# Stick-breaking heads with queries on the partitions: a backward scan on VectorE in place of triangular matmuls on TensorE

## The chip, the cores and the metric

The kernel runs on one core of one Trainium2 chip. The metric is device time in microseconds of one execution; three runs of the kernel before gave 1107.64, 1107.03 and 1107.19 us, and the median, 1107.19 us, stands for it.

## The reference, cut to what matters

One layer of a hybrid encoder, for 256 tokens of width 2048, all in float32. Eight forgetting-attention heads and eight stick-breaking heads (128 wide each) share one input projection; their outputs are normed per group and projected back; then a convolutional FFN follows (up-projection to 2 x 5632, causal depthwise convolution, SiLU gate, down-projection). The change touches the stick-breaking heads alone:

```python
def stick_breaking_attention(q, k, v):
    # beta[t,s] = sigmoid(q_t.k_s/sqrt(d)); A[t,s] = beta[t,s] * prod_{s<j<t}(1-beta[t,j]), s < t
    z = jnp.einsum('bhqd,bhkd->bhqk', q, k) * HEAD_DIM ** -0.5
    mask = k_pos[None, :] < q_pos[:, None]
    log_beta = jax.nn.log_sigmoid(z)
    log_one_minus = jnp.where(mask, log_beta - z, 0.0)
    suffix = lax.cumsum(log_one_minus, axis=key_axis, reverse=True) - log_one_minus
    weights = jnp.where(mask, jnp.exp(log_beta + suffix), 0.0)
    return jnp.einsum('bhqk,bhkd->bhqd', weights, v)
```

Each query needs, for every key, the sum of softplus(z) over all later keys up to the query. Which axis lies on the partitions decides how that sum can be taken.

## The kernel before, in words

**Arithmetic.** Every large product is made of three matmuls: a float32 matrix is split into a rounded high part and a low remainder, and high x high, high x low and low x high are summed. So each 1 MB tile of weights (128 x 2048 per tile) is loaded by a DMA into `w_raw`, its high part is written by ScalarE (`w_hi`, line 201), and its low part by VectorE (`w_lo`, line 202), before TensorE multiplies with both. `w_hi` and `w_lo` have two buffers each in the first half of the kernel, so ScalarE can write a new `w_hi` only when TensorE has read the one two tiles back.

**Order.** A projection is a run of such blocks: 24 matmuls for `token_major` (lines 231 to 241), 32 for `from_features`. After each block the host-side `step()` (line 181) advances the first two generators in the queue `waiting`; each generator is one head, cut into pieces by its `yield`s. So the small work of the heads is recorded between the blocks of whichever projection runs then. A scheduler places the recorded instructions on the engines in the section up to line 790, and each engine then works through its own queue in order.

**The forgetting heads** (`fox_head`, line 591) have queries on the partitions: scores in `ps_s`, softmax, and in a later piece three transposes by TensorE into `ps_p` (line 624), which are evacuated by ScalarE twice (lines 627 and 628) and by VectorE once (629) to make the weights `pT`; then `weighted` (line 575) multiplies with the values into `ps_o`, and `attended` (line 336) scales and splits `ps_o` into `oT` and adds its squares to `ssq`.

**The stick-breaking heads** (`sb_head`, line 701; heads 0 to 7 in this text) have keys on the partitions. The scores `ps_z` take three matmuls of 256 columns for the first 128 keys and one of 128 for the last 128 keys (lines 707 and 708). ScalarE makes log(1+exp(-|z|)) in three steps (712 to 714), VectorE makes softplus `sp` (718, 719), both split it (721, 722). After a `yield`, four matmuls with a constant triangle and a constant of -1 (lines 727 and 728) add minus the sum over later keys to the scores in place; ScalarE takes the exponential (730), and the result is already transposed the way `weighted` wants it; it is masked and split (732 to 736). After a second `yield` comes `weighted`. Two `yield`s, three pieces.

**Banks and buffers that tie the pieces together.** `ps_s`, `ps_z` and `ps_p` share one pool of two buffers (`pss`). `ps_o` shares a pool of two (`psb`, tag `t`) with `pg` (line 775, the sum of squares for a group's norm). The accumulators of all projections share a pool of two (`psa`, tag `acc`). The values of the second half of the stick-breaking heads, heads 4 to 7, are projected into one of these accumulators and then evacuated by `values` (line 522): ScalarE writes `vB` and `vBt` (line 292), VectorE writes `vBlo` (line 526). `vB`, `vBlo` and `vBt` have one buffer each, so they cannot be written before `weighted` of head 3 has read the values of heads 0 to 3.

**What runs beside the heads.** Heads 0 to 3 run under the value projection of the second half and the first blocks of the output projection; heads 4 to 7 under the output projection of the first group (`w_out`, lines 762 to 789, four column groups c = 0 to 3 of two blocks each). `finish()` (line 765) drains the heads before the second group. The output projection's c = 1 takes the accumulator that held the values of heads 4 to 7. The last `w_out` blocks are followed by the FFN, whose order is written out by hand.

Of the kernel before, what the change touches and what calls it, by code (L numbers as in the profile page):

```python
# [8 lines left out]
F32 = mybir.dt.float32  # L9
# [5 lines left out]
P = 128  # L15
D = 2048
S = 256
# [12 lines left out]

C_ID, C_TRI, C_ONE = (P * i for i in range(3))
C_MF = 3 * P
C_MS, C_NTRI, C_NONE = (C_MF + P * i for i in range(1, 4))
C_COLS = C_MF + 4 * P

AHEAD = 200
WINDOW = 2
# [8 lines left out]
def hybrid_layer(  # L46
# [31 lines left out]
    def f32(t):  # L78
        return t.bitcast(F32)
# [198 lines left out]
    with ExitStack() as actx:  # L278
# [200 lines left out]
        mask2, limit2 = (  # L479
            f32(masksR[:, i * P : (i + 1) * P]).unsqueeze(1).to_broadcast([P, 2, P]) for i in range(2)  # L480
        )
        limit = f32(masksR[:, P : 2 * P])
        gq = const.tile([P, 1], F32, name="gq")
        dve.tensor_scalar(gq, g_q, QSCALE, None, op0=ALU.mult)

# [99 lines left out]
        def weights_tiles(name):  # L585
# [2 lines left out]
                tmp.tile([P, P], F32, name=f"{name}1", tag="pT1"),  # L588
            )

        def fox_head(h, qT, kT, first):
            while any(g in waiting for g in first):
                yield
            yield
            ps = pss.tile([P, 3, P], F32, name="ps_s", tag="s")
            s0, s1 = ps[:, 0, :], ps[:, 1:3, :].rearrange("p a b -> p (a b)")
            j = h % 4
            nc.tensor.matmul(s0, qT[0][0][:, j, :], kT[0][0][:, j, :], start=True, stop=False)
# [23 lines left out]
            pt = pss.tile([P, 3, P], F32, name="ps_p", tag="s")  # L622
            for i in range(3):
                nc.tensor.transpose(pt[:, i, :], pr[:, i, :], ident)
            pT, pT1 = weights_tiles("pT")
            pt0 = pt[:, 0:2, :].rearrange("p a b -> p (a b)")
            act.copy(pT[:, 0], pt0)
            act.copy(pT1, pt[:, 2, :])
            dve.tensor_tensor(pT[:, 1], pt0, f32(pT[:, 0]), op=ALU.subtract)
            yield  # L630
            attended(weighted(vA, slice(h * HD, (h + 1) * HD), (pT, pT1)), h, g_fox, 0)

        for half in range(2):
            if half:
# [20 lines left out]
        def sb_heads(c0, scale, parts):  # L655


            heads = []
            for i in range(0, 4, 2):
                acc = feature_major(wi, c0 + i * P, psa, "acc")  # L660
                t2 = summed(tmp, acc, "t2", bufs=1)
                dve.scalar_tensor_tensor(
                    t2, t2, scale, R1.unsqueeze(1).to_broadcast([P, 2, S]), op0=ALU.mult, op1=ALU.mult
                )
                full, hi, lo = parts(i)
                some = t2[:, :, : hi.shape[2]]
                act.copy(hi, some)
                act.copy(full, t2[:, :, P:])
# [7 lines left out]
        def sb_queries(half):  # L676
            places = []

            def parts(i):
                if not places:  # L680

                    assert scored[:4] == [0, 1, 2, 3]
                    lows = last_rows("q1_low", 2) if half else [low[:, 0, 4 * P * j : 4 * P * (j + 1)] for j in range(2)]
                    places.extend((full_tile(f"qB{half}_1"), high_tile(f"qB{half}"), lows))
                full, hi, lows = places
                return full[:, i : i + 2, :], hi[:, i : i + 2, :], lows[i // 2].rearrange("p (h s) -> p h s", h=2)

            return sb_heads(B0 + 512 * half, QSCALE, parts)

        def sb_keys(half):  # L690
            places = []

            def parts(i):
                if not places:
                    two = last_rows("k1_parts", 2) if half else [low[:, 0, 4 * P * j : 4 * P * (j + 1)] for j in (2, 3)]
                    places.extend((full_tile(f"kB{half}_1"), *(of_four(t) for t in two)))
                return tuple(o[:, i : i + 2, :] for o in places)

            return sb_heads(B0 + WF + 512 * half, 1.0, parts)

        def sb_head(h, qT, kT, v):
            (q1, *q), (k1, *k) = qT[h % 4], kT[h % 4]
            ps = pss.tile([P, 3, P], F32, name="ps_z", tag="s")
            z0, z1 = ps[:, 0:2, :].rearrange("p a b -> p (a b)"), ps[:, 2, :]
            zz = ps.rearrange("p a b -> p (a b)")
            mm = nc.tensor.matmul
# [4 lines left out]
            e = tmp.tile([P, 3 * P], F32, name="e", tag="pr")  # L711
            act.activation(e, zz, AF.Abs)
            act.activation(e, e, AF.Exp, scale=-1.0)
            act.activation(e, e, AF.Ln, bias=1.0)
            sp = tmp.tile([P, 3, P], F32, name="sp", tag="sp", bufs=1)
            diagonal = sp[:, 0::2, :]
            sp = sp.rearrange("p a b -> p (a b)")
            dve.scalar_tensor_tensor(sp, zz, 0.0, e, op0=ALU.max, op1=ALU.add)
            dve.tensor_tensor(diagonal, diagonal, limit2, op=ALU.min)
            sps = tmp.tile([P, 2, 3 * P], F32R, name="sps", tag="sps")  # L720
            act.copy(sps[:, 0, :], sp)
            dve.tensor_tensor(sps[:, 1, :], sp, f32(sps[:, 0, :]), op=ALU.subtract)
            yield

            for i in range(2):
                s = sps[:, i, :]
                mm(zz, ntri[:, :P], s, start=False, stop=False, skip_group_check=True)
# [381 lines left out]
def _constants():  # L1109
# [4 lines left out]
    c[:, C_ID : C_ID + P] = i == j  # L1114
    c[:, C_TRI : C_TRI + P] = i <= j
    c[:, C_ONE : C_ONE + P] = 1.0
    c[:, C_NTRI : C_NTRI + P] = np.where(i >= j, -1.0, 0.0)
    c[:, C_NONE : C_NONE + P] = -1.0
    c[:, C_MF : C_MF + P] = np.where(j > i, BIG, 0.0)
    c[:, C_MS : C_MS + P] = np.where(i >= j, 0.0, -BIG)  # L1120
    return c


# [30 lines left out]
```

## Time and profile before

| what | value |
|---|---|
| median of three runs | 1107.19 us (1107.03 to 1107.64) |
| span of the profiled execution | 1104.9 us |
| TensorE (PE) busy | 1099.6 us, 100% |
| VectorE (DVE) busy | 870.4 us, 79% |
| ScalarE (ACT) busy | 706.3 us, 64% |
| GpSimd (POOL) busy | 44.0 us, 4% |
| DMA moved | 246.09 MB, mean 223 GB/s |
| stick-breaking heads | from about 264 to 346 us of the span |

The span is that of one execution taken by the hardware profiler, from its first instruction to its last; the run's own time is 2.3 us longer than the span at the median. Busy shares are averages over all stages. TensorE matmuls are pipelined, so their records overlap; the time a group takes on TensorE is read from the start of its first record to the start of what follows.

### The profile page before, as it was taken

The numbers are of one execution on the slowest core, as the hardware profiler recorded it, in microseconds if no ns is written. First come the engines' busy times: TensorE is split into PE (matmuls) and PEld (weight loads), VectorE is DVE, ScalarE is ACT, GpSimd is POOL, SyncE is SP. The second block draws the span as 40 slices with busy tenths as digits, with TensorE's granted clock in tenths as the row PEclk, the third lists the DMA queues.
The fourth block names the chain that finished last, engine by engine and source line by source line (L and its number), as shares of the span: only waits on it lengthen the run. The fifth ranks groups of instructions, "written<-read, shape, count | busy, mean of one in ns | idle before, by whom it ended". The sixth has DMA issues, their size and how long they took to land. (4 is left out here: it accounts for less than half of the span.)

```text
span 1104.9 us, 14836 instructions
## 1 busy us (share of the span) xinstructions
PE 1099.6 (100%) x5880; PEld 953.9 (86%) x5880; DVE 870.4 (79%) x941; ACT 706.3 (64%) x879; POOL 44.0 (4%) x44
## 2 busy tenths in 40 slices
PE   9999999999999999999999999999999999999998
PEld 7998888888888888888888888888888888888887
DVE  6755767667676677679889888889798889889896
ACT  6543555457674567667767776667676677677753
POOL 0000000000000000000000010100000010100010
PEclk9999999999999999999999999999999999999999
DMA  8776555555644396557989597986979689987985
GB/s 285 195 232 229 187 164 180 173 170 169 242 156 158 114 304 200 190 189 195 301 210 323 191 229 264 260 269 178 315 210 306 213 218 281 245 264 196 324 212 168
DMA packets 179407, 246.09 MB, mean 223 GB/s; under 512 B 4432, under 2 KB 118890, under 8 KB 179082
## 3 DMA queue, kind: packets, MB, share of 16 engines
q1 hardware_dynamic: 162458, 209.87, 58.3%
q0 software_dynamic: 16560, 34.75, 16.7%
q8 instruction: 46, 0.75, 0.3%
q10 hardware_dynamic: 320, 0.53, 0.1%
q14 instruction: 23, 0.19, 0.0%
HBM read 243.02 MB, written 2.11 MB: 222 GB/s over the span
## 5 line engine op out<-in xcount | busy, mean ns | idle before, releaser
L202 DVE TENSOR_TENSOR w_lo<-w_raw,w_hi 128x2048 fp32r<-128x2048 f32 (+1 forms) x196 | 439.7, 2246 | 155.0 <-ACT w_hi L201 153.2
L201 ACT CAST w_hi<-w_raw 128x2048 fp32r<-128x2048 f32 (+1 forms) x196 | 367.1, 1875 | 247.4 <-PE pu L250 68.9
L250 PE MATMUL pu<-hT,w_hi 128*128 128x512 f32 x1664 | 396.7, 390 | 0.0
L250 PEld LDWEIGHTS pu<-hT,w_hi 128*128 128x128 f32 x1664 | 309.4, 188 | 62.6
L257 PEld LDWEIGHTS pu<-hT,w_lo 128*128 128x128 f32 x1664 | 213.7, 191 | 8.3
L257 PE MATMUL pu<-hT,w_lo 128*128 128x256 f32 x1664 | 216.4, 283 | 0.0
L223 PE MATMUL acc<-w_hi,hT 128*128 128x512 f32 (+1 forms) x576 | 124.9, 369 | 0.0
L223 PEld LDWEIGHTS acc<-w_hi,hT 128*128 128x128 f32 x576 | 101.2, 188 | 14.2
L201 ACT CAST w_hi<-w_sum 128x2048 fp32r<-128x2048 f32 x30 | 57.2, 1908 | 42.0 <-PE pu L250 35.8
L202 DVE TENSOR_TENSOR w_lo<-w_sum,w_hi 128x2048 fp32r<-128x2048 f32 x30 | 68.7, 2290 | 19.0 <-ACT w_hi L201 19.0
L851 ACT ACTIVATE tap<-up,ccol 128x256 f32<-128x256 f32 x176 | 74.6, 495 | 0.0
L223 PE MATMUL acc<-w_lo,hT 128*128 128x512 f32 (+1 forms) x288 | 64.6, 366 | 0.0
L223 PEld LDWEIGHTS acc<-w_lo,hT 128*128 128x128 f32 x288 | 51.6, 188 | 7.5
L956 POOL DMA_DIRECT2D w_sum<-in_w_down_dram x20 | 25.7, 1284 | 742.8 <-DVE w_lo L202 732.1
L223 PE MATMUL acc<-w_hi,oT 128*128 128x512 f32 x192 | 46.5, 394 | 0.0
L223 PEld LDWEIGHTS acc<-w_hi,oT 128*128 128x128 f32 x192 | 35.4, 188 | 7.2
L223 PE MATMUL bank_a<-w_hi,s 128*128 128x512 f32 x160 | 40.1, 392 | 0.2 <-DVE x L933 0.2
L223 PE MATMUL bank_a<-w_hi,g 128*128 128x512 f32 x160 | 40.0, 392 | 0.0
L223 PE MATMUL bank_b<-w_hi,s 128*128 128x512 f32 x160 | 40.0, 392 | 0.0
L223 PEld LDWEIGHTS bank_a<-w_hi,s 128*128 128x128 f32 x160 | 28.8, 189 | 5.8 <-issue 0.6
L223 PEld LDWEIGHTS bank_a<-w_hi,g 128*128 128x128 f32 x160 | 28.9, 189 | 5.3
L223 PEld LDWEIGHTS bank_b<-w_hi,s 128*128 128x128 f32 x160 | 28.9, 189 | 5.2
(215 smaller groups left out, 1077.5 us busy)
## 6 DMA issues: line engine op xcount, KB each, us to landing
w_raw<-in_w_up_dram SPq DMA_DIRECT2D x88, 1024.0 KB, 7.9
w_raw<-in_w_down_dram SPq DMA_DIRECT2D x44, 1024.0 KB, 6.6
w_raw<-in_w_in_dram SPq DMA_DIRECT2D x36, 1024.0 KB, 5.3
w_sum<-in_w_down_dram POOLq DMA_DIRECT2D x20, 1024.0 KB, 10.3
w_raw<-in_w_out_dram SPq DMA_DIRECT2D x16, 1024.0 KB, 5.1
w_raw<-in_w_down_dram POOLq DMA_DIRECT2D x10, 1024.0 KB, 14.7
w_raw<-in_w_in_dram SPq DMA_DIRECT2D x12, 688.0 KB, 4.3
w_raw<-in_w_in_dram SPq DMA_DIRECT2D x6, 512.0 KB, 7.1
```

Of the source, the lines that this page charges most:

```text
L201: act.copy(hi[:, :n], raw[:, :n])
L202: dve.tensor_tensor(lo[:, :n], raw[:, :n], f32(hi[:, :n]), op=ALU.subtract)
L223: nc.tensor.matmul(o, lhs(i, l, t), r[:, i, :], start=starts and j == 0, stop=stops and j == 3 * n - 1, skip_group_check=more,)
L250: nc.tensor.matmul(acc[:, j, :], hi[:, i, j * P : (j + 1) * P], hT[:, k].rearrange("p a b -> p (a b)"), start=k == 0, stop=False,)
L257: nc.tensor.matmul(acc[:, j, S:], lo[:, i, j * P : (j + 1) * P], hT[:, k, 0, :], start=False, stop=k == KT - 1,)
L851: act.activation(taps[w][:, j, :], u[:, j, w : w + S], AF.Copy, scale=ccol[:, w, f : f + 1])
L956: nc.gpsimd.dma_start(mem[into][:, : nk * 512].rearrange("p (a b) -> p a b", a=nk), src, accum_op=ALU.add)
```

## The change

Scores are now made with queries on the partitions, as in the forgetting heads: one matmul of 128 columns for the first 128 queries against the first 128 keys, and three of 256 columns for the last 128 queries against all keys. In this layout the three 128 x 128 tiles of scores lie side by side as 384 columns, and the sum over later keys runs along the columns. VectorE takes it with one scan that walks the 384 columns backwards, with a factor `go_on` that is 1 everywhere and 0 at column 127, where the next query tile begins, so that the sum restarts there. VectorE subtracts the scan from the scores, ScalarE takes the exponential, VectorE masks. Two `yield`s later three TensorE transposes turn the weights around, through the same code as in the forgetting heads (now a function of its own, `transposed_weights`), and one `yield` after that `weighted` follows. A head has three `yield`s and four pieces instead of two and three. The four matmuls with the constant triangle, their split operand `sps` and the two constants are gone; the constants are loaded as a tile of 256 columns instead of 512, without a rounded copy; which of queries and keys is kept in full, high and low parts is exchanged; GpSimd fills `go_on` once.

```diff
-        masks = late.tile([P, 4 * P], F32, name="masks", tag="raw", bufs=4)
+        masks = at.tile([P, 2 * P], F32, name="masks")
         load_parameters(masks)
...
-        masksR = at.tile([P, 4 * P], F32R, name="masksR")
-        dve.tensor_copy(masksR, masks)
-        ntri = masksR[:, 2 * P :]
...
+        go_on = at.tile([P, 3 * P], F32, name="go_on")
+        nc.gpsimd.memset(go_on, 1.0)
+        nc.gpsimd.memset(go_on[:, P - 1 : P], 0.0)
...
+        def transposed_weights(e, name):
+            pt = pss.tile([P, 3, P], F32, name="ps_p", tag="s")
+            for i in range(3):
+                nc.tensor.transpose(pt[:, i, :], e[:, i, :], ident)
+            w, w1 = weights_tiles(name)
+            pt0 = pt[:, 0:2, :].rearrange("p a b -> p (a b)")
+            act.copy(w[:, 0], pt0)
+            act.copy(w1, pt[:, 2, :])
+            dve.tensor_tensor(w[:, 1], pt0, f32(w[:, 0]), op=ALU.subtract)
+            return w, w1
...
         def sb_head(h, qT, kT, v):
...
-            of_parts(z0, k, q, True, False)
-            mm(z1, k1, q1, start=False, stop=True)
+            nc.tensor.matmul(ps[:, 0, :], q0, k0, start=True, stop=False)
+            of_parts(ps[:, 1:3, :].rearrange("p a b -> p (a b)"), q, k, False, True)
...
-            sps = tmp.tile([P, 2, 3 * P], F32R, name="sps", tag="sps")
-            act.copy(sps[:, 0, :], sp)
-            dve.tensor_tensor(sps[:, 1, :], sp, f32(sps[:, 0, :]), op=ALU.subtract)
-            yield
-
-            for i in range(2):
-                s = sps[:, i, :]
-                mm(zz, ntri[:, :P], s, start=False, stop=False, skip_group_check=True)
-                mm(ps[:, 1, :], ntri[:, P:], s[:, 2 * P :], start=False, stop=i == 1, skip_group_check=True)
-            e = tmp.tile([P, 3, P], F32, name="e", tag="pr")
-            act.activation(e, ps, AF.Exp)
-            w, w1 = weights_tiles("w")
-            dve.tensor_tensor(e[:, 0, :], e[:, 0, :], limit, op=ALU.min)
-            e0 = e[:, 0:2, :].rearrange("p a b -> p (a b)")
-            act.copy(w[:, 0], e0)
-            dve.tensor_tensor(w1, e[:, 2, :], limit, op=ALU.min)
-            dve.tensor_tensor(w[:, 1], e0, f32(w[:, 0]), op=ALU.subtract)
+
+            dve.tensor_tensor_scan(
+                backwards(after), backwards(go_on), backwards(sp), 0.0, op0=ALU.mult, op1=ALU.add
+            )
+            dve.tensor_tensor(flat, zz, after, op=ALU.subtract)
+            act.activation(flat, flat, AF.Exp)
+            diagonal = e[:, 0::2, :]
+            dve.tensor_tensor(diagonal, diagonal, limit2, op=ALU.min)
+            yield
+            yield
+            w, w1 = transposed_weights(e, "w")
             yield
             attended(weighted(v, slice((h % 4) * HD, (h % 4 + 1) * HD), (w, w1)), h, g_sb, 1)
```

More of the change, by code (lines that the diff above doesn't have):

```diff
@@ L32 @@
 C_MF = 3 * P
-C_MS, C_NTRI, C_NONE = (C_MF + P * i for i in range(1, 4))
-C_COLS = C_MF + 4 * P
+C_MS = C_MF + P
+C_COLS = C_MF + 2 * P
 AHEAD = 200
@@ L475, in hybrid_layer @@
         columns(pcol, prow, 50)
-        masksR = at.tile([P, 4 * P], F32R, name="masksR")
-        dve.tensor_copy(masksR, masks)
-        ntri = masksR[:, 2 * P :]
         mask2, limit2 = (
-            f32(masksR[:, i * P : (i + 1) * P]).unsqueeze(1).to_broadcast([P, 2, P]) for i in range(2)
+            masks[:, i * P : (i + 1) * P].unsqueeze(1).to_broadcast([P, 2, P]) for i in range(2)
         )
-        limit = f32(masksR[:, P : 2 * P])
+        go_on = at.tile([P, 3 * P], F32, name="go_on")
+        nc.gpsimd.memset(go_on, 1.0)
+        nc.gpsimd.memset(go_on[:, P - 1 : P], 0.0)
         gq = const.tile([P, 1], F32, name="gq")
@@ L621, in fox_head @@
             yield
[L622 to L629, printed above, removed]
+            w = transposed_weights(pr, "pT")
             yield
-            attended(weighted(vA, slice(h * HD, (h + 1) * HD), (pT, pT1)), h, g_fox, 0)
+            attended(weighted(vA, slice(h * HD, (h + 1) * HD), w), h, g_fox, 0)
         for half in range(2):
@@ L665, in sb_heads @@
                 full, hi, lo = parts(i)
-                some = t2[:, :, : hi.shape[2]]
+                some = t2[:, :, S - hi.shape[2] :]
                 act.copy(hi, some)
-                act.copy(full, t2[:, :, P:])
+                act.copy(full, t2[:, :, :P])
                 dve.tensor_tensor(lo, some, f32(hi), op=ALU.subtract)
@@ L682, in parts @@
                     assert scored[:4] == [0, 1, 2, 3]
[L683 to L686, printed above, removed]
+                    two = last_rows("q1_parts", 2) if half else [low[:, 0, 4 * P * j : 4 * P * (j + 1)] for j in (2, 3)]
+                    places.extend((full_tile(f"qB{half}_0"), *(of_four(t) for t in two)))
+                return tuple(o[:, i : i + 2, :] for o in places)
             return sb_heads(B0 + 512 * half, QSCALE, parts)
@@ L694, in parts @@
                 if not places:
-                    two = last_rows("k1_parts", 2) if half else [low[:, 0, 4 * P * j : 4 * P * (j + 1)] for j in (2, 3)]
-                    places.extend((full_tile(f"kB{half}_1"), *(of_four(t) for t in two)))
-                return tuple(o[:, i : i + 2, :] for o in places)
+                    lows = last_rows("k1_low", 2) if half else [low[:, 0, 4 * P * j : 4 * P * (j + 1)] for j in range(2)]
+                    places.extend((full_tile(f"kB{half}_0"), high_tile(f"kB{half}"), lows))
@@ L699, in sb_keys, with backwards @@
+                full, hi, lows = places
+                return full[:, i : i + 2, :], hi[:, i : i + 2, :], lows[i // 2].rearrange("p (h s) -> p h s", h=2)
             return sb_heads(B0 + WF + 512 * half, 1.0, parts)
+        def backwards(t):
+            n = t.shape[1]
+            end = t[:, n - 1 :]
+            return bass.AP(tensor=end.tensor, offset=end.offset, ap=[list(end.ap[0]), [-1, n]])
         def sb_head(h, qT, kT, v):
-            (q1, *q), (k1, *k) = qT[h % 4], kT[h % 4]
+            (q0, *q), (k0, *k) = qT[h % 4], kT[h % 4]
@@ L712, in sb_head @@
[L712 to L719, printed above, removed]
-            sps = tmp.tile([P, 2, 3 * P], F32R, name="sps", tag="sps")
@@ L731, in sb_head @@
[L731 to L736 removed]
+            e = tmp.tile([P, 3, P], F32, name="e", tag="pr")
+            flat = e.rearrange("p a b -> p (a b)")
+            act.activation(flat, zz, AF.Abs)
@@ new lines, in sb_head @@
+            act.activation(flat, flat, AF.Exp, scale=-1.0)
+            act.activation(flat, flat, AF.Ln, bias=1.0)
+            sp, after = (
+                tmp.tile([P, 3 * P], F32, name=name, tag=name, bufs=1) for name in ("sp", "after")
+            )
+            diagonal = sp.rearrange("p (a b) -> p a b", a=3)[:, 0::2, :]
+            dve.scalar_tensor_tensor(sp, zz, 0.0, flat, op0=ALU.max, op1=ALU.add)
+            dve.tensor_tensor(diagonal, diagonal, limit2, op=ALU.min)
+            dve.tensor_tensor_scan(
+                backwards(after), backwards(go_on), backwards(sp), 0.0, op0=ALU.mult, op1=ALU.add
+            )
@@ L1116, in _constants @@
     c[:, C_ONE : C_ONE + P] = 1.0
-    c[:, C_NTRI : C_NTRI + P] = np.where(i >= j, -1.0, 0.0)
-    c[:, C_NONE : C_NONE + P] = -1.0
     c[:, C_MF : C_MF + P] = np.where(j > i, BIG, 0.0)
-    c[:, C_MS : C_MS + P] = np.where(i >= j, 0.0, -BIG)
+    c[:, C_MS : C_MS + P] = np.where(j >= i, 0.0, -BIG)
     return c
```

3 lines of the change are left out of this document (removed).

## The prediction

> **What bounds the kernel now.** I read the page first (busy times), then the windows, then the waits, then the timelines of single engines over the stretch where the change lies. From the page, and of the windows the stretch with heads 1 to 7:
>
> ```profile
> span 1104.9 us, 14836 instructions
> PE 1099.6 (100%) x5880; PEld 953.9 (86%) x5880; DVE 870.4 (79%) x941; ACT 706.3 (64%) x879; POOL 44.0 (4%) x44
> ...
> 300.00:350.00 50.00, 50.00 (x251) 42.52 (x250) 35.09 (x58) 32.38 (x48) 0.00 (x0) 1.00 0.50 172
> ```
>
> The window's columns after the stretch are its length, then busy time of PE, PEld, DVE, ACT and POOL, the granted clock and the DMA share. TensorE is busy 50.00 of 50 us at full clock; VectorE has 14.9 us to spare, ScalarE 17.6. The list of waits of TensorE begins with
>
> ```profile
> PE idle L372 <- DVE zeros L362: 1.1, 1, 1.1
> ```
>
> (total, times, longest, in us): its longest wait is at the very start. So TensorE sets the end everywhere. A microsecond of matmuls removed is a microsecond of time, and a microsecond that TensorE is made to wait is one too: nothing behind it is slower and could swallow it. Work added to VectorE and ScalarE costs nothing as long as TensorE never waits for it. Two questions follow: how much TensorE time goes, and whether TensorE now waits somewhere.
>
> **TensorE's own work.** The timeline of TensorE (start, busy, line, tile, count); a group lasts from its start to the next row's start:
>
> ```profile
> 290.69 0.33 PE L727 MATMUL ps_z<-sps,masksR 128*128 128x384 f32 x1
> ...
> 291.20 0.34 PE L513 MATMUL ps_z<-qB,low 128*128 128x256 f32 x1
> ...
> 297.83 0.42 PE L727 MATMUL ps_z<-sps,masksR 128*128 128x384 f32 x1
> ...
> 298.43 3.88 PE L223 MATMUL acc<-w_hi,oT 128*128 128x512 f32 x16
> ...
> 303.97 0.41 PE L581 MATMUL ps_o<-w,vB 128*128 128x256 f32 x2
> ...
> 304.47 0.36 PE L513 MATMUL ps_z<-qB,k_parts 128*128 128x256 f32 x1
> ...
> 305.05 3.92 PE L223 MATMUL acc<-w_hi,oT 128*128 128x512 f32 x16
> ```
>
> The four triangular matmuls of a head take 0.51 us (290.69 to 291.20) or 0.60 (297.83 to 298.43): 0.56 on average. The weighted sum takes 0.50, the scores 0.58. What replaces the triangle is in the trace, in the forgetting heads:
>
> ```profile
> 141.26 0.40 PE L581 MATMUL ps_o<-pT,vA 128*128 128x256 f32 x2
> ...
> 141.84 0.49 PE L624 MATMUL ps_p<-cs,pr 128*128 128x128 f32 x3
> 142.08 3.89 PE L223 MATMUL acc<-w_hi,hT 128*128 128x512 f32 x16
> ```
>
> Three transposes take 0.24 us, and the weighted sum ahead of them 0.58 instead of 0.50, which half the heads will have. The scores are as many matmuls of the same sizes in another order: nothing. Per head 0.56 - 0.24 - 0.04 = 0.28; eight heads: **-2.2 us**.
>
> Against that the heads come in four pieces instead of three, and each interruption of the long runs costs something:
>
> ```profile
> 123.95 3.81 PE L223 MATMUL acc<-w_hi,hT 128*128 128x512 f32 x16
> ...
> 129.42 0.38 PE L598 MATMUL ps_s<-kA,qA 128*128 128x128 f32 x2
> ...
> 350.34 3.79 PE L223 MATMUL acc<-w_hi,oT 128*128 128x512 f32 x16
> ...
> 355.78 3.79 PE L223 MATMUL acc<-w_hi,hT 128*128 128x512 f32 x16
> ```
>
> An undisturbed block lasts 5.44 us (350.34 to 355.78), one behind transposes or weighted sums 5.54 (298.43 to 303.97), one behind forgetting-style scores alone 5.47 (123.95 to 129.42). In the built program's order I count 18 interruptions by these heads instead of 13, and the transposes of x for the FFN are split at two more places: seven more, of which three are scores alone. 4 x 0.10 + 3 x 0.03 = **+0.5 us**.
>
> **Where TensorE will wait.** The extra piece moves every weighted sum of a head one block later. In the built program the weighted sum of head 3 now stands behind the last block of the output projection's c = 0, directly ahead of c = 1, with these in a row on TensorE: weighted sum of head 2, transposes of head 3, `pg`, scores of head 4, first score matmul of head 5, weighted sum of head 3, the rest of head 5's scores, the c = 1 block. Three of them wait:
> (a) head 5's scores need the `pss` buffer that head 3's transposes have just filled, so they wait until VectorE has written the low part of head 3's weights;
> (b) head 3's weighted sum takes the `psb` bank of head 2's, whose last reader is ScalarE's square `osq` of head 2, which ScalarE has behind the three steps of head 4's softplus;
> (c) c = 1 takes the accumulator with the values of heads 4 to 7, and these can be evacuated only into the buffers that head 3's weighted sum reads: after it come ScalarE's `vB` and `vBt`, then VectorE's `vBlo`, then c = 1.
> Before, head 3's weighted sum ran at 303.97, one block ahead of the first block that needed the bank, and (c) was hidden under that block. Now nothing stands between. The durations, ScalarE and then VectorE, all from this stretch; and three rows of `ps_p` (min/median/max in ns) for the evacuation of transposed weights; and TensorE's `pg`:
>
> ```profile
> 302.35 1.91 ACT L201 CAST w_hi<-w_raw 128x2048 fp32r<-128x2048 f32 x1 [1.29 <-PE acc L223]
> 304.41 0.69 ACT L292 ACTIVATE vB<-acc,rstd 128x512 fp32r<-128x512 f32 x1 [0.15 <-PE ps_o L581]
> 305.00 0.68 ACT L292 ACTIVATE vBt<-acc,rstd 128x512 f32<-128x512 f32 x1
> 305.57 0.47 ACT L347 ACTIVATE oT<-ps_o,pcol 128x256 fp32r<-128x256 f32 x1
> 305.92 0.50 ACT L712 ACTIVATE e<-ps_z 128x384 f32<-128x384 f32 x1
> 306.45 0.53 ACT L713 ACTIVATE e<-e 128x384 f32<-128x384 f32 x1
> 307.01 0.53 ACT L714 ACTIVATE e<-e 128x384 f32<-128x384 f32 x1
> 307.67 0.38 ACT L355 ACTIVATE osq<-ps_o 128x256 f32<-128x256 f32 x1
> ```
>
> ```profile
> 304.29 2.29 DVE L202 TENSOR_TENSOR w_lo<-w_raw,w_hi 128x2048 fp32r<-128x2048 f32 x1 [2.74 <-ACT w_hi L201]
> 306.50 0.75 DVE L526 SCALAR_TENSOR_TENSOR vBlo<-acc,rstd,vB 128x512 fp32r<-128x512 f32 x1
> 307.16 0.48 DVE L348 SCALAR_TENSOR_TENSOR oT<-ps_o,pcol,oT 128x256 fp32r<-128x256 f32 x1
> 307.57 0.56 DVE L718 SCALAR_TENSOR_TENSOR sp<-ps_z,e 128x384 f32<-128x384 f32 x1
> 308.09 0.42 DVE L356 TENSOR_TENSOR ssq<-ssq,osq 128x256 f32<-128x256 f32 x1
> 308.43 0.42 DVE L719 TENSOR_TENSOR sp<-sp,masksR 128x256 f32<-128x256 f32 x1
> 309.43 0.56 DVE L722 TENSOR_TENSOR sps<-sp,sps 128x384 fp32r<-128x384 f32 x1 [0.58 <-ACT sps L721]
> ```
>
> ```profile
> L627 ACT CAST pT<-ps_p x8: 350/362/365, 136.5 to 258.7; 128x256 fp32r<-128x256 f32 x8
> L628 ACT COPY pT<-ps_p x8: 258/273/282, 136.8 to 259.0; 128x128 f32<-128x128 f32 x8
> L629 DVE TENSOR_TENSOR pT<-ps_p,pT x8: 404/414/420, 138.1 to 261.1; 128x256 fp32r<-128x256 f32 x8
> ```
>
> ```profile
> 311.76 0.50 PE L777 MATMUL pg<-cs,ssq 128*128 128x1 f32 x4
> 312.13 3.92 PE L223 MATMUL acc<-w_hi,oT 128*128 128x512 f32 x16
> ```
>
> Let the last block of c = 0 start at 0. TensorE reaches the weighted sum of head 2 at 5.54, the transposes at 6.12, `pg` (0.37) at 6.36, head 4's scores (0.58) at 6.73, and is ready for head 5's at 7.31.
> (a) ScalarE starts the next `w_hi` when the block's 16 high matmuls are read, at 3.92 (302.35 against 298.43), and ends at 5.83. VectorE's `w_lo`, ahead of everything else in its queue, then runs to 8.15, `oT` of head 2 (0.48) to 8.6, the low part of head 3's weights (0.41) to 9.0; ScalarE's `oT` and two copies are done by 7.4. Head 5's first matmul starts at 9.0 instead of 7.31: a wait of 1.7 us.
> (b) ScalarE's softplus of head 4 begins when its scores are in, at 7.5, and takes 0.50 + 0.53 + 0.53 with small gaps, to 9.1; `osq` to 9.5. Head 3's weighted sum, due at 9.15, starts at 9.5: 0.4 us more. It ends at 10.0 (its last record at 10.3), head 5's other scores at 10.4.
> (c) `vB` runs from 10.0 to 10.7, `vBt` to 11.35. VectorE meanwhile does head 4's `sp` (9.1 to 9.7), the sum of squares (to 10.1), the mask (to 10.5), and then the scan, which its queue puts ahead of `vBlo`.
>
> **The scan** is not in the trace. It does two operations on 384 columns. One pass over two operands of that size costs 0.56 us (the `sp` row), two passes 1.12. I take 1.12, since each column needs the result of the one before and the two steps cannot run side by side as in the other rows; both ends stay in the range. [...]
>
> With 1.12 the scan ends at 11.6, `vBlo` (0.75) at 12.4; with 0.56 `vBt` decides and `vBlo` ends at 12.1. TensorE wanted c = 1 at 10.4: a wait of 2.0 (1.7). Together (a), (b), (c): 1.7 + 0.4 + 2.0 = **+4.1 us** (3.8 with the fast scan).
>
> **The rest.** Following the same queues on, heads 4 and 5 have two blocks between pieces and TensorE does not wait. Heads 6 and 7 are scored just ahead of the drain, and their transposes and weighted sums are threaded between matmuls of the second group; by the same durations TensorE arrives there within 0.1 us of the data: **+0.1 us**, and whatever the scan takes beyond 1.12 adds there. In the earlier half (heads 0 to 3) two us and more remain. VectorE does per head 0.56 + 0.42 + 1.12 + 0.56 + 0.42 + 0.41 = 3.5 us instead of about 2.5: 8 us over 85, covered by the idle time above. The larger constants' rounding copy, once on VectorE, goes, in a stretch where it is hidden anyway; the constants' DMA is half as large and goes out ahead of two weight loads instead of behind them, on SP's queue. GpSimd fills `go_on` between the two steps that make the identity:
>
> ```profile
> 0.74 0.20 POOL L363 MEMSET cs<- 128x128 f32 x1 [0.29 <-POOLq L1139]
> ...
> 3.97 0.23 PE L129 MATMUL pp<-cs,prow 16*128 16x16 f32 x1
> ```
>
> Three times the columns is some 0.6 us, and the identity's first use is at 3.97: hidden; without that cover it would cost 0.6.
>
> **Sum**, against the profiled execution's span: 1104.9 - 2.2 + 0.5 + 4.1 + 0.1 = 1107.4; with the 2.3 us around the span that the median of 1107.19 has, **1109.7 us**, slower by 0.23%. 0.2%, or 2.2 us, is about what a measurement of this kernel can tell from no change, so this stands near its edge.
>
> **Rivals.**
> 1. *The waits at c = 1 are covered* (not slower). Waits (a) and (c) hang on the `w_lo` split standing ahead of head 3's work on VectorE. If head 3's low part is written before TensorE arrives at 7.31, (a) is gone and (b), (c) shrink by what ScalarE then does earlier; it decides from about 1.7 us. For it: VectorE's 14.9 idle us. Against: its queue is in order and `w_lo` cannot start before 5.83. With no wait left: 1107.2 - 2.2 + 0.5 = 1105.5 us.
> 2. *The scan is much slower.* At the price of the longest VectorE row above (2.29 us, that of 2048 columns) (c) grows by 1.2 us and head 6's or 7's transposes wait about as long: 1112.1 us. Against: 384 columns only.
> 3. *TensorE's clock falls.* The waits break a stretch that has none now. For: transposes and waits replace dense matmuls. Against: the granted clock is 1.00 in the quoted window, and the forgetting heads' transposes leave the blocks behind them at 5.54. One block at half clock would add 5.5 us: 1115 us. [...]
>
> **How the numbers follow.** The forecast gets 0.62, with its own range 1108.2 to 1111.2: one of the three waits less, or the scan and the interruptions at their dear ends; two thirds of it lie above 1109.4, the edge of "slower". Rival 1 gets 0.14 (most of it within 0.2%), rival 2 0.14, rival 3 0.06, the rest, 0.04, is split. Slower: 0.41 + 0.14 + 0.06 = 0.61. Same: 0.21 + 0.10 + 0.02 = 0.33. Faster: 0.06. The range takes in the forecast, rival 2 and the partly covered cases: 1107.0 to 1112.4; rival 3 and full cover are left out.
>
> **What would show it.** Right: in the waits of TensorE a row of 1 to 2 us each at the first score matmul of head 5 behind VectorE's low weights, and at `acc` behind `vBlo`; transposes of `e` at 0.24 us for three; granted clock 1.00; a scan of 0.6 to 1.2 us. Wrong: no TensorE wait near 310 us (rival 1), waits at `ps_p` on the mask step (rival 2), or blocks longer than 5.6 us (rival 3).

## The result and the profile after

| | before | after |
|---|---|---|
| median of five runs | 1107.19 us (1106.93 to 1107.64) | 1111.79 us (1109.35 to 1112.69) |
| ratio | | 1.0036, 95% interval 1.0025 to 1.0046 |
| span of the profiled execution | 1104.9 us | 1108.0 us |

The changed kernel is slower by 0.36%. Its runs fall into two groups: two at a granted clock of 1.00 for the whole span (1109.35 and 1109.79 us, the profiled one among them) and three at 0.997 or 0.998 (1111.79, 1112.34 and 1112.69). The forecast was 1109.7.

The page of the changed kernel, the same window as before, and all of TensorE's waits over 0.1 us (in each row the total, how often, the longest):

```profile
span 1108.0 us, 14825 instructions
PE 1099.6 (99%) x5872; PEld 951.8 (86%) x5872; DVE 876.2 (79%) x940; ACT 702.5 (63%) x879; POOL 44.4 (4%) x46
```

```profile
300.00:350.00 50.00, 47.03 (x232) 39.28 (x231) 34.60 (x49) 27.61 (x41) 0.00 (x0) 1.00 0.57 198
```

```profile
PE acc L223 <- DVE vBlo L525: 1.5, 1, 1.5
PE ps_z L714 <- DVE w L599: 1.3, 1, 1.3
PE idle L372 <- DVE zeros L362: 1.1, 1, 1.1
PE bank_a L223 <- ACT w_hi L201: 1.0, 1, 1.0
PE ps_o L580 <- ACT osq L355: 0.2, 1, 0.2
PE ps_h L298 <- DVE r L118: 0.2, 1, 0.2
```

TensorE was busy 50.00 of these 50 us; now it is busy 47.03. The missing 2.97 us are three waits that stood nowhere in the list of before: at `ps_z`, at `ps_o` and at the `acc` of line 223. (The kernel before has the waits at `idle` and `ps_h` too, with the same 1.1 and 0.2 us.) VectorE, the engine that got the new work, is at 34.60 busy us in this window against 35.09 before: it is not full, TensorE waits for single steps of it. (The wait at `bank_a` lies near the end, in the FFN. Over the profiles of this study it is between nothing and 2.5 us: up to 0.5 in the four without the change, from 0 to 2.5 in the ten with it.) The three waits in TensorE's timeline, with two rows from a block earlier (three transposes and what follows them), and VectorE's and ScalarE's steps that end the waits:

```profile
301.73 0.49 PE L594 MATMUL ps_p<-cs,e 128*128 128x128 f32 x3
301.97 3.91 PE L223 MATMUL acc<-w_hi,oT 128*128 128x512 f32 x16
...
309.36 0.28 PE L512 MATMUL ps_z<-kB,q_parts 128*128 128x256 f32 x1
310.93 0.49 PE L714 MATMUL ps_z<-kB,qB 128*128 128x128 f32 x2 [1.29 <-DVE w L599]
311.60 0.50 PE L580 MATMUL ps_o<-w,vB 128*128 128x256 f32 x2 [0.18 <-ACT osq L355]
...
312.52 0.28 PE L512 MATMUL ps_z<-kB,q_parts 128*128 128x256 f32 x1
314.29 3.93 PE L223 MATMUL acc<-w_hi,oT 128*128 128x512 f32 x16 [1.49 <-DVE vBlo L525]
```

```profile
310.46 0.41 DVE L599 TENSOR_TENSOR w<-ps_p,w 128x256 fp32r<-128x256 f32 x1
...
312.63 0.96 DVE L730 TENSOR_TENSOR_SCAN after<-go_on,sp 128x384 f32<-128x384 f32 x1
313.51 0.73 DVE L525 SCALAR_TENSOR_TENSOR vBlo<-acc,rstd,vB 128x512 fp32r<-128x512 f32 x1
```

```profile
311.18 0.37 ACT L355 ACTIVATE osq<-ps_o 128x256 f32<-128x256 f32 x1
312.14 0.69 ACT L292 ACTIVATE vB<-acc,rstd 128x512 fp32r<-128x512 f32 x1 [0.27 <-PE ps_o L580]
312.72 0.68 ACT L292 ACTIVATE vBt<-acc,rstd 128x512 f32<-128x512 f32 x1
```

The wait in brackets counts from the modelled end of the last matmul; from row to row the first gap is 310.93 - 309.36 = 1.57 us where a score matmul takes 0.12, so 1.45, and the last is 314.29 - 312.52 - 0.12 = 1.65. With some 0.5 at `ps_o` the three are 3.6 us.

How much the heads cost in all is read between two rows that both kernels have: the last weighted sum of the forgetting heads, and the first matmul of the FFN. Before, then after:

```profile
264.06 0.40 PE L581 MATMUL ps_o<-pT,vA 128*128 128x256 f32 x2
...
397.05 1.98 PE L250 MATMUL pu<-hT,w_hi 128*128 128x512 f32 x8
```

```profile
264.05 0.40 PE L580 MATMUL ps_o<-pT,vA 128*128 128x256 f32 x2
...
399.42 1.98 PE L250 MATMUL pu<-hT,w_hi 128*128 128x512 f32 x8
```

132.99 us before, 135.37 after: +2.38 us. Of this 3.6 are waits, so the rest became 1.2 us shorter. The profiled spans differ by more, 3.1 us; the other 0.7 lie behind the second row, where the wait at `bank_a` is 1.0 us after and 0.2 before. The starts, 264.06 and 264.05, also show that `go_on` and the moved constants cost nothing ahead of the heads.

### The profile page after: what moved, and what is told of

The parts are those of the page before. It is cut to its first block, busy times and chain, and to the rows that moved or that the text cites. A ratio compares the mean times of both kernels' runs of the same rounds, so it can differ in the third digit from the quotient of the medians.

```text
span 1108.0 us, 14825 instructions
## 1 busy us (share of the span) xinstructions
PE 1099.6 (99%) x5872; PEld 951.8 (86%) x5872; DVE 876.2 (79%) x940; ACT 702.5 (63%) x879; POOL 44.4 (4%) x46
```

## The experiments

All experiments but the plain repeats change one thing against the kernel that they are set beside. Times are medians; "before" is the kernel before, run beside them on the same chip.

**The changed kernel again.** Why are some runs 2 to 3 us longer?

> The changed kernel once more. Its five runs fell into two groups: 1109.35 and 1109.79 us at a mean granted clock of 1.0, and 1111.79 to 1112.69 us at 0.997 to 0.998. Theory: the waits of TensorE ahead of the output projection's c = 1 (1.3, 0.2 and 1.5 us in the profile) let the clock be lowered for a stretch in some executions. Then the runs fall into the same two groups again, and a profile taken in the slower group shows a granted clock under 1.0 in the stretch behind 310 us and nowhere else. Rival: the slower group comes from somewhere else in the kernel or from the chip at that hour; then the low clock lies elsewhere, or the kernel before shows it too.

Measured: 1111.92 us (1111.70 to 1112.44), ratio 1.0046 (1.0033 to 1.0058); all five executions at 0.996 or 0.997. The three waits are as in the first profile, and now there is a trace with the lower clock. Its windows (the last three numbers are the granted clock, the DMA share and GB/s), and the c = 1 block:

```profile
307.50:311.00 3.50, 2.51 (x20) 2.23 (x18) 2.77 (x3) 2.53 (x6) 0.00 (x0) 1.00 0.63 238
311.00:314.30 3.30, 1.68 (x10) 1.29 (x10) 2.94 (x9) 2.97 (x9) 0.00 (x0) 0.90 0.81 247
314.30:318.00 3.70, 3.34 (x8) 2.66 (x9) 3.70 (x10) 1.96 (x5) 0.00 (x0) 0.50 0.16 63
318.00:322.00 4.00, 4.00 (x14) 3.15 (x13) 2.00 (x4) 0.69 (x1) 0.00 (x0) 0.69 0.00 0
322.00:326.00 4.00, 4.00 (x19) 3.29 (x18) 2.63 (x2) 1.64 (x2) 0.00 (x0) 1.00 0.00 0
```

```profile
314.66 6.61 PE L223 MATMUL acc<-w_hi,oT 128*128 128x512 f32 x16 [1.50 <-DVE vBlo L525]
321.12 2.00 PE L223 MATMUL acc<-w_lo,oT 128*128 128x512 f32 x8
```

Full clock up to the third wait, half clock in the block right behind it, full clock again before 322. Taken as 1.00 or 0.50 in one stretch, the windows put the 0.50 from 313.6, within the third wait (0.10 x 3.3 / 0.5 = 0.7 us ahead of 314.3), to 320.5 (0.31 x 4.0 / 0.5 = 2.5 us behind 318): 6.8 us, an estimate. The 16 high matmuls take 321.12 - 314.66 = 6.46 us instead of the 3.8 of other blocks: 2.7 us lost. A third set of the same kernel, beside later experiments:

> The changed kernel once more, so that the next three have its clock on the same chip. Theory: the three waits of TensorE (1.3, 0.2 and 1.5 us) are in every execution, and most executions have the granted clock at about 0.5 for some 7 us right behind them; 1109.4 without the lower clock, 1111.5 to 1112.5 with it.

Measured: 1111.57 us (1108.97 to 1117.43), six executions, two of them at 1.00 (1108.97 and 1109.76). The profiled one, 1117.43, has the lower clock, a wait of 2.5 us at `bank_a`, and reached the heads 2 us late; what delayed it there is not known. In its timeline the clock falls earlier: the weighted sum of head 3, ahead of the third wait, already has matmuls of 0.41 us where others have 0.28.

```profile
314.27 0.41 PE L580 MATMUL ps_o<-w,vBlo 128*128 128x256 f32 x1
...
316.67 5.98 PE L223 MATMUL acc<-w_hi,oT 128*128 128x512 f32 x16 [0.93 <-DVE vBlo L525]
```

The gaps of 1.3 and 0.2 us alone were followed by it here: by its windows (0.99 from 311 to 314.3, 0.50 to 318, 0.61 to 322) for 6.9 us at 0.50. The mean clock of this execution, 0.995 over 1115.7 us, makes 10 to 12 us, so there is more of it. The lone gap of 2.5 us at `bank_a` has slow matmuls behind it. The third set, then the kernel before (min/median/max in ns, first and last start):

```profile
L223 PE MATMUL bank_a<-w_hi,s x160: 389/389/628, 536.3 to 1093.4; 128*128 128x512 f32 x160
...
L223 PE MATMUL bank_a<-w_lo,s x80: 389/389/628, 538.1 to 1095.1; 128*128 128x512 f32 x80
```

```profile
L223 PE MATMUL bank_a<-w_hi,s x160: 387/389/467, 529.4 to 1083.9; 128*128 128x512 f32 x160
...
L223 PE MATMUL bank_a<-w_lo,s x80: 389/389/395, 531.2 to 1084.8; 128*128 128x512 f32 x80
```

The longest take 0.63 us, against 0.47 and 0.40 before, and from the last high matmul to the last low one it is 1.7 us against 0.9. Over the three sets 12 of 16 executions had the lower clock (3, 5 and 4).

**Buffers of their own for the values of heads 4 to 7**, in space of the forgetting heads that is free by then. By the prediction's (c), c = 1 waits because these values could only go where head 3's weighted sum still reads.

```diff
-        vA = (at.tile([P, WF], F32R, name="vA"), vA_low, at.tile([P, WF], F32, name="vA_t1"))
+        vA = (at.tile([P, WF], F32R, name="vA", tag="vA"), vA_low, at.tile([P, WF], F32, name="vA_t1", tag="vA_t1"))
...
-                for name, dt, tag in (("vB", F32R, "vB"), ("vBlo", F32R, "minus_c0"), ("vBt1", F32, "vBt1"))
+                for name, dt, tag in (
+                    ("vB", F32R, ("vB", "vA")[half]), ("vBlo", F32R, f"minus_c{half}"), ("vBt1", F32, ("vBt1", "vA_t1")[half])
+                )
```

> The changed kernel with buffers of their own for the values of heads 4 to 7 (in tiles that the forgetting heads no longer use), so that they are evacuated without waiting for head 3's weighted sum. Theory: wait (c) goes, and with it (a) and (b), since head 3's weighted sum can stand behind a block again; TensorE's own saving shows alone. The region between the heads' start and the FFN grew by 2.4 us with 3.6 us of waits in it, so 1.2 us are saved: 1106.0 us (1105.5 to 1106.4), all runs at clock 1.0 and within 0.5 us of each other. Rival (the transposes, the scan or the extra interruptions cost the time, the waits only stand where it shows): 1108 us or more, with the waits in another place.

Measured: 1105.66 us (1105.23 to 1106.17), ratio 0.9988 (0.9979 to 0.9997), clock 1.00 in all eleven executions. All three waits are gone, not (c) alone. Between the same two rows:

```profile
264.17 0.40 PE L580 MATMUL ps_o<-pT,vA 128*128 128x256 f32 x2
...
308.94 3.94 PE L223 MATMUL acc<-w_hi,oT 128*128 128x512 f32 x16
...
314.53 0.41 PE L580 MATMUL ps_o<-w,vB 128*128 128x256 f32 x2
...
395.89 1.98 PE L250 MATMUL pu<-hT,w_hi 128*128 128x512 f32 x8
```

131.72 us, 1.27 less than before. In this kernel's timeline the c = 1 block starts at 308.94, right behind `pg`, and head 3's weighted sum (314.53) and head 4's scores come after it, with a whole block between them and whatever they need. So the shared buffers had done more than delay `vBlo`: with c = 1 held back by head 3, the weighted sum of head 3 and the scores of heads 4 and 5 had all been put ahead of it, next to one another.

**The extra piece without the scan.** The kernel before, with one more `yield` and nothing else:

```diff
             dve.tensor_tensor(w[:, 1], e0, f32(w[:, 0]), op=ALU.subtract)
             yield
+            yield
             attended(weighted(v, slice((h % 4) * HD, (h % 4 + 1) * HD), (w, w1)), h, g_sb, 1)
```

> The kernel before with one more yield ahead of each stick-breaking head's weighted sum: the arithmetic, the triangular matmuls and the three engines' work as before, only the pieces come one block later as in the changed kernel. Theory: the later weighted sum of head 3 alone makes the wait, so TensorE waits by 3 to 4 us in the same place and the time is 1110 to 1111.5 us, with some runs 2 to 3 us above that from the clock. Rival (scan and transposes make the wait): 1107.2 us, no wait.

Measured: 1113.0 us (1112.10 to 1113.82), ratio 1.0056 (1.0043 to 1.0068). Neither scan nor transposes, and slower than the change itself:

```profile
PE ps_z L727 <- ACT sps L721: 1.9, 1, 1.9
...
PE ps_o L581 <- DVE rs_a L112: 0.9, 1, 0.9
PE acc L223 <- DVE vBlo L526: 0.2, 1, 0.2
```

```profile
314.30:318.00 3.70, 2.77 (x8) 2.12 (x9) 3.30 (x6) 1.04 (x3) 0.00 (x0) 0.73 0.48 188
318.00:322.00 4.00, 4.00 (x16) 3.22 (x15) 0.00 (x0) 0.69 (x1) 0.00 (x0) 0.82 0.00 0
```

The later order is enough for 3.0 us of waits in the same stretch, and the clock falls behind them here too. But they are not the same three waits: two end by other steps, the first step on `pg` (`rs_a`) and the split of the softplus (`sps`), and only 0.2 us are left at `vBlo`. The same kernel with the values in buffers of their own:

> The kernel before with the extra yield ahead of the weighted sum (as in the earlier run, which took 1113.0) and with buffers of their own for the values of heads 4 to 7. Theory, that the extra piece costs its time only through those buffers: no wait of TensorE over 0.3 us from 300 to 350 us, clock 1.00, 1107.0 to 1107.6, that is 0.1 to 0.6 above the kernel before for the extra interruptions. Rival, that a piece more costs by itself (later weighted sums pile up on ScalarE and VectorE): 1109 or more.

Measured: 1107.71 us (1107.13 to 1108.07) against 1106.79, ratio 1.0009 (1.0000 to 1.0017), no TensorE wait over 0.2 us but the one at the start:

```profile
264.07 0.40 PE L581 MATMUL ps_o<-pT,vA 128*128 128x256 f32 x2
...
398.03 1.98 PE L250 MATMUL pu<-hT,w_hi 128*128 128x512 f32 x8
```

133.96 us, 0.97 more than before without a wait. TensorE's timeline shows 25 interruptions of the blocks here against 17 before, so each costs about 0.12 us if they cost all of it. That is above the 0.1 to 0.6 expected; the rival (1109 or more) is out.

**The buffers alone, and the scan twice.** Do the buffers bring something by themselves, and what does the scan cost the end?

> The changed kernel with buffers of their own for the values of heads 4 to 7, once more, as the ground for the next two: 1105.2 to 1106.0, clock 1.00, no wait of TensorE over 0.5 us between 300 and 350 us.

> The kernel before with the same buffers of their own. The difference to own_beside is then the change without the collision at c = 1. Theory: TensorE never waited there before, so nothing changes against the kernel before, 1106.6 to 1107.3, and own_beside is 1.2 to 1.6 us below it: TensorE's own saving less the extra interruptions. Rival: the buffers themselves bring something (c = 1 can start earlier in the list), then before_own is 1106 or less and the change without the collision is worth under 0.8 us.

> own_beside with every scan done twice, 0.96 us more of VectorE's time for each of the eight heads. Theory: VectorE has some ten idle us in this stretch and nobody waits for it, so the time is that of own_beside within 0.5 us; at most a wait of up to 1 us at the transposes of head 6 or 7, scored just ahead of the drain. Rival, that the scan is on the path of each head: 8 x 0.96 = 7.7 us more, 1113.

```diff
-            dve.tensor_tensor_scan(
-                backwards(after), backwards(go_on), backwards(sp), 0.0, op0=ALU.mult, op1=ALU.add
-            )
+            for _ in range(2):
+                dve.tensor_tensor_scan(
+                    backwards(after), backwards(go_on), backwards(sp), 0.0, op0=ALU.mult, op1=ALU.add
+                )
```

Measured, with 1107.23 us for before: the kernel before with the buffers 1107.19 (1106.82 to 1107.45), so they bring nothing by themselves, as expected; the changed kernel with the buffers 1106.34 (1105.70 to 1109.63), ratio 0.9996 (0.9987 to 1.0005); with two scans 1106.59 (1105.89 to 1109.66). Between the two rows the changed kernel with the buffers takes 131.73 us, as in its first set. But three of its eleven runs took 1108.25 to 1109.63, which is higher than expected, and two of these had a clock of 0.998, as had one of the kernel with two scans (1109.66). No trace of those was taken, and their cause stays open; in the traces of these kernels no gap is longer than 0.4 us but the one at the start. One execution of the kernel before, too, took 1109.07, at full clock. So the gain over before is 1.27 us in the traces and 0.9 to 1.25 at the medians where 1.2 to 1.6 was expected, and in one of the two sets the interval takes in no gain at all. The doubled scan put 7.7 us more on VectorE and 0.25 us on the median:

```profile
L731 DVE TENSOR_TENSOR_SCAN after<-go_on,sp x16: 945/957/958, 268.6 to 352.2; 128x384 f32<-128x384 f32 x16
```

```profile
PE ps_p L594 <- DVE e L737: 0.3, 1, 0.3
```

The only wait in this stretch is at the transposes of a head scored just ahead of the drain, where the prediction had put it.

**The wait made longer.** The changed kernel with `vBlo` written four times in the second half:

> The changed kernel with VectorE's low part of the values of heads 4 to 7 written four times instead of once, which makes wait (c) 2.0 us longer (3 x 0.67) and changes nothing else. Theory that the wait itself lowers the clock: the full-clock time is 1109.6 + 2.0 = 1111.6 us, and now most or all runs are in the lowered group, at 1113.5 to 1116 us, with a profile that shows a granted clock under 1.0 right behind the wait. Rival that the groups have nothing to do with the wait: the same share of runs in each group, both 2.0 us later.

Measured: 1116.19 us (1115.17 to 1117.63), ratio 1.0085 (1.0071 to 1.0099). The wait grew by 3.8 us where three extra writes of 0.7 would make it about 2, because other VectorE work was queued between the copies (the last two of the four):

```profile
PE acc L223 <- DVE vBlo L526: 5.3, 1, 5.3
```

```profile
316.43 0.75 DVE L526 SCALAR_TENSOR_TENSOR vBlo<-acc,rstd,vB 128x512 fp32r<-128x512 f32 x1
317.10 0.74 DVE L788 SCALAR_TENSOR_TENSOR x<-acc,rg,x 128x512 f32<-128x512 f32 x1
317.75 0.74 DVE L526 SCALAR_TENSOR_TENSOR vBlo<-acc,rstd,vB 128x512 fp32r<-128x512 f32 x1
```

The end moved by 4.3 us against 1111.92, of which the longer wait is 3.8; the rest may be the wait at `bank_a`, 0.7 in this profile and absent in that one. So a microsecond of TensorE's wait is a microsecond of time here. How often the lower clock comes can't be read from this run, since all four executions had it, as most had without the longer wait. It lasted longer: by the windows (0.91 from 311 to 314.3, 0.50 to 322, 0.76 to 326) 10.2 us at 0.50 in this trace, against 6.8 and 6.9 there in the two traces of the changed kernel that have it.

**TensorE kept at work.** If idle time lowers the clock, needless work in the wait should keep it up. The changed kernel with 14 matmuls that nobody reads, behind head 3's weighted sum:

```diff
             attended(weighted(v, slice((h % 4) * HD, (h % 4 + 1) * HD), (w, w1)), h, g_sb, 1)
+            if h == 3:
+                fill = psb.tile([P, S], F32, name="fill", tag="t")
+                for i in range(14):
+                    nc.tensor.matmul(fill, oT[0][:, 0, :P], oT[0][:, 0, :], start=i == 0, stop=i == 13)
```

> The changed kernel with 14 more matmuls of 256 columns (1.6 us at 0.12 us each) directly behind head 3's weighted sum, into a PSUM tile that nobody reads: TensorE works where it waited for vBlo, and the c = 1 block starts within 0.2 us of where it did. If it is TensorE's idle time that lowers the clock, the lower clock is gone or shorter (the wait behind head 3's low weights, 1.3 us, is left): 1109.3 to 1110, clock 1.00 in the windows from 311 to 326 us. If the clock is lowered by something else in this stretch, the time stays at 1111.5 to 1112.5 and the windows show 0.5 again.

> The changed kernel with TensorE kept at work during the wait for vBlo, once more. So far four of its five executions had the full clock (1109.5 to 1110.4) and one took 1112.9; of sixteen of the changed kernel eleven had the lower clock. If the idle time lowers the clock, most executions are again at 1109.3 to 1110.5 at a granted clock of 1.00. If the first five were chance, about two in three are at 1111 to 1113 at 0.996 to 0.998.

Measured: 1109.77 us (1109.48 to 1112.91) in five executions, ratio 1.0033 (1.0021 to 1.0045), then 1109.72 (1109.35 to 1111.08) in nine, ratio 1.0024 (1.0014 to 1.0034). The first set's profile, TensorE's timeline and windows:

```profile
312.01 0.51 PE L580 MATMUL ps_o<-w,vB 128*128 128x256 f32 x2 [0.18 <-ACT osq L355]
...
312.62 1.92 PE L745 MATMUL fill<-oT 128*128 128x256 f32 x14
...
314.70 3.94 PE L223 MATMUL acc<-w_hi,oT 128*128 128x512 f32 x16
```

```profile
311.00:314.30 3.30, 2.78 (x21) 2.59 (x22) 2.94 (x9) 2.85 (x8) 0.00 (x0) 1.00 0.81 242
314.30:318.00 3.70, 3.70 (x18) 3.00 (x18) 3.33 (x9) 0.91 (x2) 0.00 (x0) 1.00 0.18 68
```

The c = 1 block starts 2.69 us after the weighted sum, exactly as in the changed kernel (314.29 - 311.60), so the filler hid nothing else. Now 3 of 14 executions have a clock of 0.998, against 12 of 16 without the filler (the expectation above says eleven). On the one chip where both ran side by side it is 1 of 5 against 4 of 6; the second set had no changed kernel beside it. One of the three has a profile, in the second set:

```profile
311.00:314.30 3.30, 3.12 (x14) 2.93 (x15) 2.78 (x7) 2.54 (x7) 0.00 (x0) 0.58 0.93 291
314.30:318.00 3.70, 3.70 (x22) 3.29 (x21) 3.24 (x9) 0.91 (x2) 0.00 (x0) 0.91 0.06 24
```

There the clock is 1.00 in the window up to 311, which holds the first wait, the one that is left (1.3 us; TensorE is busy for 2.20 of its 3.50), and the two rows make 3.4 us at 0.50 behind it (0.42 x 3.3 and 0.09 x 3.7 us, over 0.5). So with less idle time in these few us the lower clock came less often, and wherever the windows show it, it stands behind gaps; the kernel before, without such gaps (its longest, 1.1 us, is at the start), never had 0.998 or less beside any of the experiments. Whether a given execution gets it is not settled by the kernel alone: the first profile of the changed kernel has the same three gaps at full clock.

**One piece less.** The changed kernel with one `yield` between scan and transposes, so three pieces to a head:

```diff
             dve.tensor_tensor(diagonal, diagonal, limit2, op=ALU.min)
             yield
-            yield
             w, w1 = transposed_weights(e, "w")
```

> The changed kernel with one yield instead of two between the scan and the transposes, so three pieces to a head as before. If the count of pieces alone put head 3's weighted sum behind the last block of c = 0, the wait behind vBlo is gone and the time is 1105.5 to 1106.5. Rival, from the queues of the built program: the transposes and the weighted sum of a head come together between two blocks, VectorE's w_lo stands between them, and head 3's weighted sum is still directly ahead of c = 1; then the wait behind vBlo is 2 to 3.3 us, with four to six waits of 0.1 to 0.4 us at weighted sums, and the time 1109 to 1113.

Measured: 1111.89 us (1110.52 to 1112.60), ratio 1.0044 (1.0031 to 1.0057), four of five executions at 0.998. The wait did not go, it doubled, and the waits at weighted sums did not come:

```profile
PE acc L223 <- DVE vBlo L525: 3.1, 1, 3.1
```

Head 3's transposes and weighted sum (306.53 and 307.51 in its timeline) come ahead of `pg`, inside the last block of c = 0, some three us before its end. This wait has another reason: VectorE's queue has a step for `pg` and a `w_lo` (2.29 us in the kernel before) ahead of `vBlo`, and VectorE was busy for 0.42 of the 3.50 us from 307.5 to 311; `pg` came at 310.77. The count of pieces alone does not decide it.

## Why the prediction was right

**The bound and the direction.** TensorE set the end throughout: 3.6 us of waits at full clock in place of none, and the end moved with them. VectorE's 7.7 us more cost 0.25 us in the doubled scan.

**TensorE's own work, -2.2.** The change without waits is -1.27 between the two rows, and the extra piece alone +0.97, so the exchange of triangles for transposes is about -2.2 (the extra piece stood at another place in that experiment, so this is an estimate). Three transposes take 301.97 - 301.73 = 0.24 us, the row of the forgetting heads.

**Interruptions, +0.5, mis-sized.** They cost about 1.0 by the extra piece alone. There are more of them where nothing makes the pieces bunch up (26 against 17 in the kernel with its own buffers, 24 in the changed kernel; I counted seven more), and each took 0.12 us rather than 0.03 to 0.10.

**The waits, +4.1.** All three are at the places named and end by the instructions named: (a) 1.45 for 1.7, (b) 0.5 for 0.4, (c) 1.65 for 2.0, in all 3.6. About half of the difference in (c) is the scan, 0.957 us instead of 1.12. `vBt` ends at 313.40 and the scan at 313.59, so the two come out nearly even and a faster scan would have gained 0.2 us at most. The two wrong sizes, +0.5 and -0.5, cancelled, which is luck: +2.4 between the rows for a sum of +2.5. The 0.7 us more that the profiled span has behind these rows stood in no term.

**The cause of (c), incomplete.** "The extra piece moves every weighted sum of a head one block later" is enough for waits of this size in this place, as the kernel before with one more `yield` shows, though with other steps at their ends; taking one piece away does not undo (c), because VectorE's order then delays `vBlo`. What ties c = 1 to head 3 is the one set of value buffers; with a second set both kernels with four pieces lose the waits.

**The scan.** 0.957 us lies between the two bounds, 0.56 and 1.12: 1.7 passes of 0.56. That the two steps take two whole passes was my estimate; the row shows less, and no run shows why.

**Rivals.** 1 (waits covered) did not happen by itself; its 1105.5 is what the kernel with its own buffers measured, 1105.66. 2 (a much slower scan) is refuted by the row. 3 (the clock falls) was given 0.06 and happened in 12 of 16 executions: this step of the prediction failed. The forecast holds for the executions at full clock, 1109.35 and 1109.79; the median of 1111.79 is one with the lower clock. It lies above the forecast's own range (to 1111.2) and inside the wider one only because that takes in rival 2's 1112.1, a case that did not happen; the lower clock had been left out of it. That is luck. I had priced a whole block at half clock, 5.5 us; it was half a block, 2.7. The changed kernel's three gaps are 1.3, 0.2 and 1.5 us, and the clock fell; in the third set it fell behind the first two, and behind a lone gap of 2.5 us matmuls took 0.63 us. That gaps this short leave the clock at 1.00, as I took it, was not shown by the trace of before, whose longest gap is 1.1 us, and does not hold here.

## What to carry to other kernels

When the pieces of a software pipeline are moved by one step, look for buffers with a single copy that tie a late reader to an early writer: here they put a full accumulator in line behind a weighted sum, and a second set of buffers took away 3.6 us of waits, more than the arithmetic that the change was about. Where TensorE is the bound, price a wait there twice: its own length, and what the clock does behind it, in the second set 1.5 us at the third wait and 2.7 us in the block behind it. And read the change's gain in a version without the waits before judging the arithmetic: it was -1.3 us between two rows of the traces here, hidden under 3.6.

## What the runs showed of the hardware that was not expected

Three idle gaps of 1.3, 0.2 and 1.5 us within about five us went with a lower granted clock in 12 of 16 executions of the same program, and with no change in the others; with the last gap filled by needless matmuls it was 3 of 14. In the windows of the traces with the lower clock no value is under 0.50. Taken as 1.00 or 0.50, they give 0.50 for 3.4 to 3.5 us in three traces (the extra piece without the scan, one piece less, the needless matmuls), for 6.8 and 6.9 in two (the changed kernel) and for 10.2 in one (the longer wait): close to one, two and three times 3.4. Neither the reason for that nor why executions of one program differ is shown by any run here. Lone gaps of 3.1 us (one piece less) and 2.5 us (the third set's `bank_a`) were followed by it, lone gaps of 1.1 us and less at `bank_a` were not.

A backward scan over 384 float32 columns, read and written with a negative step, takes 0.957 us on VectorE (0.945 to 0.958 over sixteen of them), 1.7 times an ordinary pass over two operands of that size (0.56).
